# The first block's feed-forward layers: the first pair of column tiles as eight plain products instead of seven combined ones

## The chip, the core and the metric

The kernel runs on one core of a Trainium2 chip. That core has TensorE (PE in the profile; its weight loads are shown as PEld), VectorE (DVE), ScalarE (ACT), GpSimd (POOL) and SyncE (SP), which here only starts loads from the chip's memory. Each engine works through its own queue in order and waits on semaphores for the others. The metric is the time of one execution in microseconds on the device; less is better.

## The reference, cut to what matters

Two layers of a first block (attention of two kinds, each followed by a SwiGLU feed-forward layer), then a second block that the change doesn't touch. The sequence has 512 positions, the model 1024 columns, and the hidden layer of both feed-forward layers 2816.

```python
def rmsnorm(x, g):
    xf = x.astype(F32)
    y = xf * lax.rsqrt(jnp.mean(xf * xf, axis=-1, keepdims=True) + EPS)
    return (y * g.astype(F32)).astype(x.dtype)

def swiglu(h, w_gate, w_up, w_down):
    return (jax.nn.silu(h @ w_gate) * (h @ w_up)) @ w_down

    for layer in range(DEPTH):          # DEPTH = 2
        h = rmsnorm(x, attn_norm[layer])
        ...
        h = rmsnorm(x, ffn_norm[layer])
        x = x + swiglu(h, ffn_w_gate[layer], ffn_w_up[layer], ffn_w_down[layer])
```

## The kernel before, in words

Activations lie transposed: `x[0]` to `x[7]` are eight tiles of 128 model columns by 512 positions. The function `ffn(i, edge)` does one feed-forward layer, and is called for both layers (the first at some 293 us of the span, the second at some 926 us).

**Products.** The 22 column tiles of the hidden layer are taken in `NP = 11` pairs. For one pair the weights are a 2 x 2 matrix of blocks A11, A12, A21, A22: row one or two is the first or second tile of the pair, column one or two the first or second four of the eight model tiles. A block `wg[p, b]` (b = 0 to 3 in that order) has 128 x 1024 numbers, gate and up columns together. The activations are a 2 x 2 matrix too: B11 and B21 are the model tiles 0 to 3 and 4 to 7 for positions 0 to 255, B12 and B22 the same for positions 256 to 511. The plain way is eight block products. The kernel uses a scheme with seven (Winograd's form of Strassen's), which needs sums of weight blocks and of activation blocks: its products a to g use B11, B21, T1 = B12 - B11, T2 = B22 - T1, B22, T3 = B22 - B12 and T4 = B21 - T2, in that order.

**Split numbers.** Each f32 operand is split in a high part (a cast to fp32r on ACT, line 206, tiles `h` for weights and `t` for activations) and the rest (a subtraction on DVE, line 207, tiles `l` and again `t`). A block product (`product`, line 710) is three products of the parts: 24 matmuls of 128 x 128 by 256 columns. `scaled(q)` (line 741) makes the activation block `y[q]` from x, the norm's weights and the broadcast factor `edge.r` (named `rbc` in the profile): y0 to y3 are B11, B21, B12, B22. `parts4` splits such a block in four pieces.

**Order.** PE, DVE, ACT and SP run in an order that the code writes out (`manual_schedule`). `jobs` lists the products: a and b of the pairs 0, 1 and 2 (`AHEAD = 3`) come first, then c, d, e, f of pair 0, then c, g, d, e, f with the g of the pair before, and from pair 3 on also the products with the down weights (`D`). `ahead(n + 2)` splits the weights of a job two jobs early, `pre_c`, `post_c` and `pre_e` make the sums of weight blocks (lines 806 to 815), and the dictionary `turn` says at which job the sums of activations are made:

```python
            turn = {2: sum1, 3: sum2, 4: plain, 5: sum3, 6: sum4}
            also = {0: [lambda: edge.norm(1)], 1: [lambda: edge.spread(1)]}
```

`sum1` and `sum2` scale B12 and B22 first. `edge.norm(0)` and `edge.spread(0)` have made the norm's factor of the first 256 positions before `ffn` starts; `edge.norm(1)` and `edge.spread(1)` make that of the other 256 behind the first and the second product. `norm` sums squares with small matmuls (line 68, `sums`; squares of six tiles are added on POOL into `acc`, those of the last two come from ACT), goes through a few small instructions on DVE and ACT (lines 71 to 73, 224 to 234), and `spread` broadcasts the factor (line 79 on PE, line 80 on ACT). The results of c to g are put together on DVE in lines 873 to 889 (`m` is m5, `u`, `c`), and the matmuls of f add to the bank of d, so f waits until `u` has been made from it. SiLU and the gating of the pair's four quarters are `first` (`hq`) and `others` (`hr`).

Above `ffn` stands the output projection of the mixer (`pso`, lines 174 to 176 and 521), which adds to x, first for positions 0 to 255, then for 256 to 511. Its instructions, the squares and the first instructions of `ffn` (those in `high_priority`) are interleaved by the builder.

Of the kernel before, what the change touches and what calls it, by code (L numbers as in the profile page):

```python
# [8 lines left out]
F32 = mybir.dt.float32  # L9
# [73 lines left out]
class Net:  # L83
# [631 lines left out]
    def ffn(self, i, edge):  # L715
# [5 lines left out]
        with ExitStack() as st:  # L721
# [12 lines left out]

            y, T = [place("y") for _ in range(4)], []
# [8 lines left out]
            t = [None] * 4  # L744

            def sum1():
                scaled(2)
                t[0] = place("y")
                v_.tensor_sub(out=t[0], in0=y[2], in1=y[0])
                T.append(self.parts4(t[0], piece))  # L750

            def sum2():
                scaled(3)
                t[1] = place("y")
                v_.tensor_sub(out=t[1], in0=y[3], in1=t[0])
                T.append(self.parts4(t[1], piece))

            def plain():
                T.append(self.parts4(y[3], piece))

            def sum3():
                t[2] = place("y")
                v_.tensor_sub(out=t[2], in0=y[3], in1=y[2])
                T.append(self.parts4(t[2], piece))

            def sum4():
                t[3] = place("y")
                v_.tensor_sub(out=t[3], in0=y[1], in1=t[1])
                T.append(self.parts4(t[3], piece))

# [22 lines left out]

            p1, s1, m5, u, pa, pb, cs, hq, hr, done, ws, sm = ({} for _ in range(12))
            due = {}
# [24 lines left out]
            def split(job, p):  # L820
                if job == "D":
                    r, m, x0, x1 = p
                    ws[job, p] = parts(down.pop(p), 256 * (x1 - x0))
                    return
# [33 lines left out]


            def run(job, p):  # L860
                if job == "a":
                    p1[p] = bank("p1")
                    mm(p1[p], (job, p), 0, True)
                    s1[p] = w2.tile([128, S], F32, tag="s1", name="s1", bufs=3)
                    s_.copy(out=s1[p], in_=p1[p])
                elif job == "b":
                    mm(p1[p], (job, p), 1, False)
                    later(1, lambda: first(p))
                elif job == "c":
                    pb[p] = bank("pb")  # L870
                    mm(pb[p], (job, p), 2, True)
                    m5[p] = self.sm.tile([128, S], F32, tag="rq", name="m5", bufs=1)
                    s_.copy(out=m5[p], in_=pb[p])  # L873
                    later(1, lambda: v_.tensor_tensor(out=m5[p], in0=m5[p], in1=s1[p], op=ALU.add))
                elif job == "d":
                    pa[p] = bank("pa")
                    mm(pa[p], (job, p), 3, True)
                    u[p] = w2.tile([128, S], F32, tag="u", name="u", bufs=1)
                    v_.tensor_tensor(out=u[p], in0=s1[p], in1=pa[p], op=ALU.add)
                elif job == "e":  # L880
                    mm(pb[p], (job, p), 4, False)
                    cs[p] = w2.tile([128, 3, 2, 256], F32, tag="c", name="c", bufs=1)
                    v_.tensor_tensor(out=cs[p][:, 0], in0=two(u[p]), in1=two(pb[p]), op=ALU.add)
                elif job == "f":
                    mm(pa[p], (job, p), 5, False)
                    v_.tensor_tensor(out=cs[p][:, 2], in0=two(m5[p]), in1=two(pa[p]), op=ALU.add)  # L886
                elif job == "g":
                    mm(pa[p], (job, p), 6, False)
                    v_.tensor_tensor(out=cs[p][:, 1], in0=two(s1[p]), in1=two(pa[p]), op=ALU.add)
# [17 lines left out]

            jobs = [(j, p) for j in "ab" for p in range(AHEAD)]
            rounds = [(r, min(r + ROUND, NP)) for r in range(0, NP, ROUND)]
            D = iter([("D", (r, m, *r_)) for r, r_ in enumerate(rounds) for m in range(8)])  # L910
            for p in range(NP):
                if p < AHEAD:
                    order = "cGdef"
                else:
                    order = ("acGdbefDD", "aDcGDdDbeDf", "aDcDGdbef")[p % ROUND]
                for j in order:
                    if j == "D":
                        jobs.append(next(D))
                    elif j != "G":
                        jobs.append((j, p))  # L920
                    elif p:
                        jobs.append(("g", p - 1))
# [26 lines left out]
            trig = self.trig() if i == 0 else iter(())  # L949
            with self.tc.manual_schedule(engines={ET.PE, ET.DVE, ET.Activation, ET.SP}):  # L950
# [4 lines left out]
                for p in range(AHEAD):  # L955
                    load(0, p, early)
                first_raw = []
                for p in range(AHEAD):
                    r = pw.tile([128, 1024], F32, tag=f"r{2 + p // 2}", name="r", bufs=2)
                    raw[1, p] = r  # L960
                    nc.sync.dma_start(out=r, in_=wg[p, 1])
                for n in range(2):
                    ahead(n)
                for n, (j, p) in enumerate(jobs):
                    now[0] = n
                    for fn in due.pop(n, []):
                        fn()
                    if n == 3:
                        load(3, 0)
                        load(0, 0)  # L970
                        load(2, 0)
                    if n == 4:
                        load(1, 0)
                        load(2, 1)
                    if n == 5:
                        load(3, 1)
                    ahead(n + 2)
# [1056 lines left out]
```

## Time and profile before

| | us |
|---|---|
| median of 3 runs | 2052.57 (2052.55 to 2055.12) |
| the profiled execution | 2061.09 |
| its span, first to last instruction | 2059.4 |
| PE busy in the span | 1930.6 (94%) |
| DVE busy in the span | 1360.5 (66%) |
| mean granted TensorE clock | 0.966 |

A page of the profile gives busy times per engine; the timeline lists instructions with their start and, in brackets, how long the engine stood idle before and which instruction ended that. The granted clock is 1.00 at 2.4 GHz and 0.50 at 1.2 GHz. A wide matmul (256 columns) is shown with its whole duration, some 0.28 us, though the next starts 0.12 us later, so distances between starts are what counts on PE.

### The profile page before, as it was taken

What the parts mean: (1) busy time and instruction counts of PE and PEld (TensorE: products, weight loads), DVE (VectorE), ACT (ScalarE), POOL (GpSimd) and SP (SyncE); (2) the same over time, 40 slices, a digit from 0 to 9 for tenths busy, and PEclk for the clock granted to TensorE, in tenths of its full rate; (3) what the DMA queues carried; (4) which work ended last, traced back from release to release, by engine and by line L of the source; (5) the groups of instructions that cost most, each with busy time, mean ns of one, the idle gap of its engine ahead of it and who ended that gap; (6) DMA issues with size and microseconds to landing.
All of it is one profiled execution on the core that took longest, in us unless ns stands there. A gap on an engine that the chain in (4) does not pass through costs nothing. (4 is left out here: it accounts for less than half of the span.)

```text
span 2059.4 us, 29588 instructions
## 1 busy us (share of the span) xinstructions
PE 1930.6 (94%) x11604; PEld 1642.0 (80%) x11604; DVE 1360.5 (66%) x2294; ACT 895.1 (43%) x1532; POOL 425.8 (21%) x429
## 2 busy tenths in 40 slices
PE   9969987999999999996999999979989999999997
PEld 7736677899997867776899998768878788888886
DVE  6435658867677666557877675777848678666424
ACT  5435544434444455534434343534235545444321
POOL 2314310000001165420000000444424241111001
PEclk9979998999999999998999999989989999999998
DMA  4230023323232310113333231321210222232332
GB/s 159 70 67 20 28 105 103 131 85 120 76 103 67 96 55 23 34 58 122 119 108 121 75 108 52 111 88 67 72 52 2 78 69 95 99 98 97 94 93 70
DMA packets 57987, 169.38 MB, mean 82 GB/s; under 512 B 6288, under 2 KB 13368, under 8 KB 57848
## 3 DMA queue, kind: packets, MB, share of 16 engines
q1 hardware_dynamic: 54544, 162.51, 23.9%
q10 hardware_dynamic: 3224, 4.72, 1.1%
q8 instruction: 91, 1.49, 0.3%
q14 instruction: 48, 0.39, 0.1%
q0 software_dynamic: 80, 0.26, 0.0%
HBM read 161.70 MB, written 5.77 MB: 81 GB/s over the span
## 5 line engine op out<-in xcount | busy, mean ns | idle before, releaser
L168 ACT CAST whi<-raw 128x1024 fp32r<-128x1024 f32 (+3 forms) x146 | 144.4, 990 | 282.9 <-PE o L175 93.2
L169 DVE TENSOR_TENSOR wlo<-raw,whi 128x1024 fp32r<-128x1024 f32 (+3 forms) x138 | 165.6, 1200 | 128.5 <-ACT whi L168 128.0
L710 PE MATMUL pa<-t,h 128*128 128x256 f32 x1056 | 191.2, 283 | 9.6 <-DVE c L886 4.9
L710 PEld LDWEIGHTS pa<-t,h 128*128 128x128 f32 x1056 | 163.9, 190 | 13.1 <-issue 9.6
L1005 POOL TENSOR_TENSOR acc<-acc,sqt 128x256 f32<-128x256 f32 (+1 forms) x58 | 68.5, 1182 | 505.1 <-ACT sqt L1004 503.1
L207 DVE TENSOR_TENSOR l<-r,h 128x1024 fp32r<-128x1024 f32 x104 | 127.0, 1221 | 52.5 <-ACT h L206 52.0
L710 PE MATMUL pb<-t,h 128*128 128x256 f32 x704 | 134.9, 292 | 21.4 <-ACT m L873 11.6
L710 PE MATMUL pa<-t,l 128*128 128x256 f32 x528 | 149.1, 282 | 1.3 <-DVE l L207 1.3
L710 PE MATMUL p<-t,h 128*128 128x256 f32 x704 | 131.8, 288 | 8.4 <-ACT h L206 8.4
L206 ACT CAST h<-r 128x1024 fp32r<-128x1024 f32 x104 | 107.6, 1046 | 68.1 <-PE pd L175 20.5
L175 PE MATMUL o<-xl,whi 128*128 128x512 f32 (+1 forms) x352 | 134.5, 382 | 0.9 <-DVE xl L214 0.9
L174 PE MATMUL o<-xh,whi 128*128 128x512 f32 (+1 forms) x352 | 134.7, 383 | 0.0
L710 PEld LDWEIGHTS pb<-t,h 128*128 128x128 f32 x704 | 115.5, 200 | 23.2 <-ACT m L873 12.0
L176 PE MATMUL o<-xh,wlo 128*128 128x512 f32 (+1 forms) x352 | 133.9, 381 | 0.0
L176 PE MATMUL pd<-ah,l 128*128 128x512 f32 x320 | 127.3, 398 | 1.9 <-DVE l L207 1.9
L174 PE MATMUL pd<-ah,h 128*128 128x512 f32 x320 | 126.9, 397 | 0.3 <-ACT h L206 0.3
L175 PE MATMUL pd<-al,h 128*128 128x512 f32 x320 | 126.8, 396 | 0.0
L710 PEld LDWEIGHTS p<-t,h 128*128 128x128 f32 x704 | 112.6, 195 | 10.0 <-ACT h L206 8.8
L710 PE MATMUL p<-t,l 128*128 128x256 f32 x352 | 101.5, 288 | 2.7 <-DVE l L207 2.7
L710 PE MATMUL pb<-t,l 128*128 128x256 f32 x352 | 102.6, 291 | 0.9 <-DVE l L207 0.9
L710 PEld LDWEIGHTS pa<-t,l 128*128 128x128 f32 x528 | 100.5, 190 | 2.1 <-DVE l L207 2.1
L206 ACT CAST h<-raw 128x768 fp32r<-128x768 f32 (+2 forms) x70 | 55.6, 800 | 82.6 <-PE pd L175 60.8
(545 smaller groups left out, 5211.7 us busy)
## 6 DMA issues: line engine op xcount, KB each, us to landing
r<-w_gu SPq DMA_DIRECT2D x94, 512.0 KB, 3.6
raw<-w_gu SPq DMA_DIRECT2D x50, 512.0 KB, 3.6
raw<-w_dn SPq DMA_DIRECT2D x48, 384.0 KB, 4.0
raw<-w_in SPq DMA_DIRECT2D x22, 512.0 KB, 3.5
raw<-w_dn SPq DMA_DIRECT2D x16, 448.0 KB, 3.2
raw<-w_qka SPq DMA_DIRECT2D x8, 512.0 KB, 3.6
raw<-w_dn SPq DMA_DIRECT2D x16, 256.0 KB, 2.6
raw<-w_out SPq DMA_DIRECT2D x8, 512.0 KB, 3.8
```

The lines of the kernel that those rows point to most:

```text
L168: nc.scalar.copy(out=hi[:, :n], in_=raw[:, :n])
L169: (eng or nc.vector).tensor_sub(out=lo[:, :n], in0=raw[:, :n], in1=f(hi[:, :n]))
L174: mm(out, lh, rh, start=start, stop=False)
L175: mm(out, lh, rl, start=False, stop=False)
L176: return mm(out, ll, rh, start=False, stop=stop)
L206: self.nc.scalar.copy(out=hi, in_=src)
L207: (eng or self.nc.vector).tensor_sub(out=lo, in0=src, in1=f(hi))
L710: self.nc.tensor.matmul(c, l, r, start=first and n == 0, stop=k == 3 and n == 2, skip_group_check=True)
L1005: return nc.gpsimd.tensor_add(out=self.acc[:, c], in0=self.acc[:, c], in1=t)
```

## The change

Pair 0 is computed with the eight plain block products (job `q`), so that it needs only the blocks themselves. The first twelve jobs are now the eight products of pair 0 and a, b of the pairs 1 and 2; then c, d, e, f of pair 1 follow, and the order goes on as before. B12 and B22 are scaled and split at jobs 2 and 3, and the sums T1 to T4 at jobs 4, 6, 8 and 13. The split of the first two weight blocks is put ahead of the scaling of B11 and B21 inside `high_priority`, and the loads of weights are issued in the order of the new jobs (`fetch`).

```diff
-            own = iter([(pp, f"t{j}") for j in range(12)] + [(self.xp, f"x{n}{k}") for k in range(8) for n in "hl"])
+            own = [(pp, f"t{j}") for j in range(12)] + [(self.xp, f"x{n}{k}") for k in range(8) for n in "hl"]
+            own = iter(own + own[8:12])
...
+            def quadrant(n, q):
+                scaled(q)
+                T[n] = self.parts4(y[q], piece)
...
+            def term(n, x, z):
+                t[n] = place("y")
+                v_.tensor_sub(out=t[n], in0=x(), in1=z())
+                T[n] = self.parts4(t[n], piece)
...
+            def each(n):
+                if n == 0:
+                    hq[0] = w2.tile([128, 256], F32, tag="hq", name="hq", bufs=3)
+                elif 0 not in hr:
+                    hr[0] = w2.tile([128, 3, 256], F32, tag="hr", name="hr", bufs=1)
+                gated(hr[0][:, n - 1, :] if n else hq[0], quads[n][:, 0:256], quads[n][:, 256:512])
...
+                if job == "q":
+                    _, n, q, start = p
+                    if start:
+                        quads[n] = bank("c")
+                    mm(quads[n], (job, p), q, start)
+                    if not start:
+                        later(1, lambda: each(n))
+                        if n == 3:
+                            later(3, lambda: hidden(0))
...
-            jobs = [(j, p) for j in "ab" for p in range(AHEAD)]
+            jobs = [q("A11", 0, "B11", True), q("A21", 2, "B11", True), ("a", 1), ("a", 2),
+                    q("A12", 0, "B21", False), q("A22", 2, "B21", False), ("b", 1), ("b", 2),
+                    q("A11", 1, "B12", True), q("A21", 3, "B12", True), q("A12", 1, "B22", False), q("A22", 3, "B22", False)]
...
-            for p in range(NP):
-                if p < AHEAD:
+            for p in range(1, NP):
+                if p < 3:
                     order = "cGdef"
...
-            turn = {2: sum1, 3: sum2, 4: plain, 5: sum3, 6: sum4}
+            turn = {2: lambda: quadrant("B12", 2), 3: lambda: quadrant("B22", 3),
+                    4: lambda: term("T1", lambda: y[2], lambda: y[0]), 6: lambda: term("T2", lambda: y[3], lambda: t["T1"]),
+                    8: lambda: term("T3", lambda: y[3], lambda: y[2]), 13: lambda: term("T4", lambda: y[1], lambda: t["T2"])}
...
+            fetch = {0: [lambda: block(1, 2, None, 3)], 1: [lambda: block(0, 0, None, 3, "A11")],
+                     2: [lambda: load(0, 1), lambda: block(2, 0, None, 3, "A21"), lambda: load(2, 1), lambda: load(3, 1)],
+                     5: [lambda: load(3, 2)], 9: [lambda: load(1, 1)], 10: [lambda: load(2, 2)]}
...
                 with self.tc.high_priority(HP):
-                    for q in range(2):
-                        scaled(q)
-                        T.append(self.parts4(y[q], piece))
...
+                    for n in range(2):
+                        ahead(n)
+                    quadrant("B11", 0)
+                    quadrant("B21", 1)
```

The queues show three places where this moves work. On ACT, at the end of the first mixer's projection (x_78 to x_85 are x0 to x7; the squares feed the norm of positions 0 to 255), before:

```order
L1004 ACTIVATE sqt<-x_81 128x256
L1004 ACTIVATE sqt<-x_82 128x256
L1004 ACTIVATE sqt<-x_83 128x256
L60 ACTIVATE sqt<-x_84 128x256
L60 ACTIVATE sqt<-x_85 128x256
L1001 ACTIVATE acc<-x_78 128x256
```

and now:

```order
L1017 ACTIVATE sqt<-x_81 128x256
L206 CAST h<-raw 128x1024
L1017 ACTIVATE sqt<-x_82 128x256
L1017 ACTIVATE sqt<-x_83 128x256
L206 CAST h<-raw 128x1024
L60 ACTIVATE sqt<-x_84 128x256
L60 ACTIVATE sqt<-x_85 128x256
L1014 ACTIVATE acc<-x_78 128x256
```

The casts of the first two weight blocks stand among the squares; before, three such casts stood behind the four casts of B11 and B21. DVE's subtractions of the two blocks moved in the same way, among the additions to x. On DVE, behind the scaling of B22 in the first layer (y_2448 to y_2451 are y0 to y3; the names with s and raw or r are sums of weights and weights), before:

```order
L755 TENSOR_TENSOR y_2641<-y_2451,y_2588 128x1024
L207 TENSOR_TENSOR t_2644<-y_2641,t_2643 128x512
L207 TENSOR_TENSOR t_2648<-y_2641,t_2647 128x512
L207 TENSOR_TENSOR l_2682<-s_2635,h_2681 128x1024
L810 TENSOR_TENSOR s_2635<-s_2635,r_2627 128x1024
L811 TENSOR_TENSOR r_2629<-r_2627,r_2629 128x1024
L207 TENSOR_TENSOR t_2690<-y_2451,t_2689 128x512
L207 TENSOR_TENSOR t_2694<-y_2451,t_2693 128x512
L838 TENSOR_TENSOR hq_2675<-hq_2675,p1_2502 128x256
L207 TENSOR_TENSOR l_2727<-s_2635,h_2726 128x1024
L815 TENSOR_TENSOR r_2677<-r_2677,s_2635 128x1024
```

and now:

```order
L207 TENSOR_TENSOR t_2642<-y_2451,t_2641 128x512
L207 TENSOR_TENSOR t_2646<-y_2451,t_2645 128x512
L207 TENSOR_TENSOR l_2677<-r_2466,h_2676 128x1024
L753 TENSOR_TENSOR y_2680<-y_2450,y_2448 128x1024
L207 TENSOR_TENSOR t_2683<-y_2680,t_2682 128x512
L207 TENSOR_TENSOR t_2687<-y_2680,t_2686 128x512
L207 TENSOR_TENSOR l_2719<-raw_2500,h_2718 128x1024
L826 TENSOR_TENSOR hq_2714<-hq_2714,c_2506 128x256
L207 TENSOR_TENSOR l_2750<-raw_2549,h_2749 128x1024
L753 TENSOR_TENSOR y_2753<-y_2451,y_2680 128x1024
```

The sums of pair 0's weights (lines 806 to 815) are gone there, B22 itself is split first, and T1 and T2 come later. Further on in the same queue, ahead of the `u` of pair 1, which both kernels make, before:

```order
L883 TENSOR_TENSOR c_2880<-u_2846,pb_2784 128x512
L207 TENSOR_TENSOR l_2883<-r_2625,h_2882 128x1024
L886 TENSOR_TENSOR c_2880<-m5_2809,pa_2821 128x512
L207 TENSOR_TENSOR l_2914<-s_2819,h_2913 128x1024
L815 TENSOR_TENSOR r_2772<-r_2772,s_2819 128x1024
L874 TENSOR_TENSOR m5_2943<-m5_2943,s1_2576 128x512
L207 TENSOR_TENSOR l_2947<-r_2772,h_2946 128x1024
L889 TENSOR_TENSOR c_2880<-s1_2527,pa_2821 128x512
L207 TENSOR_TENSOR l_2980<-r_2679,h_2979 128x1024
L806 TENSOR_TENSOR s_2985<-r_2817,r_2886 128x1024
L879 TENSOR_TENSOR u_3012<-s1_2576,pa_2987 128x512
L838 TENSOR_TENSOR hr_2977<-hr_2977,c_2880 128x768
```

and now:

```order
L826 TENSOR_TENSOR hr_2747<-hr_2747,c_2835 128x256
L207 TENSOR_TENSOR l_2961<-r_2861,h_2960 128x1024
L826 TENSOR_TENSOR hr_2747<-hr_2747,c_2869 128x256
L879 TENSOR_TENSOR m5_2991<-m5_2991,s1_2631 128x512
L207 TENSOR_TENSOR l_2996<-r_2586,h_2995 128x1024
L791 TENSOR_TENSOR s_3001<-r_2894,r_2716 128x1024
L753 TENSOR_TENSOR y_3003<-y_2449,y_2753 128x1024
L207 TENSOR_TENSOR t_3006<-y_3003,t_3005 128x512
L207 TENSOR_TENSOR t_3010<-y_3003,t_3009 128x512
L884 TENSOR_TENSOR u_3038<-s1_2631,pa_3013 128x512
L836 TENSOR_TENSOR al_3041<-hq_2714,ah_3040 128x256
```

T4 now stands right ahead of `u`, the three `c` of pair 0 are gone, and the gating of pair 0's other three quarters is done in three small steps (two of them above) ahead of `u` instead of one behind it.

## Rows read from the trace of the kernel before

**Rows 1.** Stretches of the first layer: length, busy per engine, granted clock, DMA share, GB/s.

```profile
293.00:362.00 69.00, 50.84 (x353) 48.83 (x351) 53.66 (x72) 29.05 (x44) 2.02 (x2) 0.85 0.34 116
362.00:400.00 38.00, 34.66 (x284) 33.95 (x285) 33.57 (x39) 19.00 (x25) 0.00 (x0) 1.00 0.39 132
400.00:660.00 260.00, 259.13 (x1718) 237.02 (x1717) 185.19 (x213) 102.25 (x131) 4.20 (x3) 1.00 0.28 91
```

**Rows 2.** Whom PE waited for, 293 to 400 us: total, times, longest.

```profile
PE pb L710 <- ACT m L873: 5.8, 1, 5.8
PE pb L710 <- ACT h L206: 4.9, 1, 4.9
PE p L710 <- ACT h L206: 4.6, 1, 4.6
```

**Rows 3.** Timeline of PE, first layer.

```profile
292.96 0.28 PE L176 MATMUL pso<-oh,wl 128*128 128x256 f32 x1
...
308.62 0.59 PE L79 MATMUL sums<-dg,ones 128*128 128x256 f32 x2
...
346.32 0.40 PE L710 MATMUL pa<-t,h 128*128 128x256 f32 x2
...
349.19 0.40 PE L710 MATMUL pb<-t,h 128*128 128x256 f32 x2
```

**Rows 4.** Timeline of ACT, both layers: small steps of the norm, casts, squares.

```profile
286.47 0.20 ACT L224 ACTIVATE rst<-v 128x2 f32<-128x2 f32 x1 [0.17 <-DVE v L71]
...
296.20 0.62 ACT L206 CAST t<-y 128x512 fp32r<-128x512 f32 x1 [0.17 <-DVE y L741]
296.73 2.94 ACT L206 CAST h<-raw 128x1024 fp32r<-128x1024 f32 x3
299.57 0.72 ACT L60 ACTIVATE sqt<-x 128x256 f32<-128x256 f32 x2
...
914.79 0.42 ACT L1004 ACTIVATE sqt<-x 128x256 f32<-128x256 f32 x1 [0.40 <-POOL acc L1005]
...
928.51 0.62 ACT L206 CAST t<-y 128x512 fp32r<-128x512 f32 x1 [0.17 <-DVE y L741]
```

**Rows 5.** The second weight block's load: issue in both layers, landing in the first.

```profile
279.94 0.33 SPq L784 DMA_DIRECT2D raw<-w_gu  x1
...
DMA to landing us min/median/max: 4.2/4.2/4.2
...
911.43 0.33 SPq L784 DMA_DIRECT2D raw<-w_gu  x1
```

**Rows 6.** Timeline of DVE, first layer, behind the `u` of pair 1.

```profile
362.04 0.95 DVE L838 TENSOR_TENSOR hr<-hr,c 128x768 f32<-128x768 f32 x1
```

**Rows 7.** Scaling of B12 to the end of pair 1's `u`, both layers; columns as in rows 1.

```profile
311.80:362.04 50.24, 37.37 (x267) 35.91 (x265) 41.73 (x53) 20.58 (x29) 0.00 (x0) 0.86 0.29 96
943.71:993.95 50.24, 36.93 (x267) 35.44 (x265) 41.73 (x52) 20.57 (x29) 0.00 (x0) 0.86 0.28 94
```

**Rows 8.** DVE in that stretch of the first layer, by form: busy, mean ns | idle before, releaser.

```profile
L207 DVE TENSOR_TENSOR l<-r,h 128x1024 fp32r<-128x1024 f32 x7 | 8.6, 1222 | 5.1 <-ACT h L206 5.0
L207 DVE TENSOR_TENSOR t<-y,t 128x512 fp32r<-128x512 f32 x10 | 6.5, 686 | 2.7 <-ACT t L206 2.7
...
L879 DVE TENSOR_TENSOR u<-s,pa 128x512 f32<-128x512 f32 x2 | 1.4, 678 | 0.0
L838 DVE TENSOR_TENSOR hq<-hq,p 128x256 f32<-128x256 f32 x3 | 1.2, 413 | 0.0
```

**Rows 9.** Timeline of PE around the first sums of squares, second layer.

```profile
915.63 0.28 PE L176 MATMUL pso<-oh,wl 128*128 128x256 f32 x1
...
917.81 0.36 PE L174 MATMUL pso<-oh,wh 128*128 128x256 f32 x1
```

**Rows 10.** Two short stretches of the second layer; columns as in rows 1.

```profile
918.00:924.00 6.00, 6.00 (x38) 5.82 (x38) 4.31 (x12) 2.16 (x7) 2.20 (x3) 0.72 0.01 4
1000.00:1002.00 2.00, 0.00 (x0) 0.00 (x0) 2.00 (x4) 0.00 (x0) 0.00 (x0) 1.00 0.54 213
```

More of the change, by code (lines that the diff above doesn't have):

```diff
@@ L732, in piece @@
                 return p_.tile([128, 2, 256], F32R, tag=tag, name="t")
-            y, T = [place("y") for _ in range(4)], []
+            y, T = [place("y") for _ in range(4)], {}
             def scaled(q):
@@ L742, in scaled @@
                                             in1=edge.r[:, c], op0=ALU.mult, op1=ALU.mult)
[L744 to L769, printed above, removed]
+            def quadrant(n, q):
+                scaled(q)
+                T[n] = self.parts4(y[q], piece)
+            t = {}
+            def term(n, x, z):
+                t[n] = place("y")
+                v_.tensor_sub(out=t[n], in0=x(), in1=z())
+                T[n] = self.parts4(t[n], piece)
             ring = self.turns({"h": [(self.wp, "whi", 2)] * 2 + [(pw, "whi", W3)] * W3,
@@ L791, in parts @@
                 return hi, lo
-            p1, s1, m5, u, pa, pb, cs, hq, hr, done, ws, sm = ({} for _ in range(12))
+            p1, s1, m5, u, pa, pb, cs, hq, hr, done, ws, sm, quads = ({} for _ in range(13))
             due = {}
@@ L823, in split @@
                     ws[job, p] = parts(down.pop(p), 256 * (x1 - x0))
+                    return
+                if job == "q":
+                    ws[job, p] = parts(raw[p[0]])
                     return
@@ L857, in others @@
                 gated(hr[p], cs[p][:, :, 0, :], cs[p][:, :, 1, :])
-            def run(job, p):
-                if job == "a":
+            def each(n):
[4 more added lines that the diff above has]
+                gated(hr[0][:, n - 1, :] if n else hq[0], quads[n][:, 0:256], quads[n][:, 256:512])
+            def run(job, p):
+                if job == "q":
+                    _, n, q, start = p
[6 more added lines that the diff above has]
+                            later(3, lambda: hidden(0))
+                elif job == "a":
                     p1[p] = bank("p1")
-                    mm(p1[p], (job, p), 0, True)
+                    mm(p1[p], (job, p), "B11", True)
                     s1[p] = w2.tile([128, S], F32, tag="s1", name="s1", bufs=3)
@@ L866, in run @@
                 elif job == "b":
-                    mm(p1[p], (job, p), 1, False)
+                    mm(p1[p], (job, p), "B21", False)
                     later(1, lambda: first(p))
@@ L880, in run @@
                 elif job == "e":
-                    mm(pb[p], (job, p), 4, False)
+                    mm(pb[p], (job, p), "B22", False)
                     cs[p] = w2.tile([128, 3, 2, 256], F32, tag="c", name="c", bufs=1)
@@ L947, in ffn, with block @@
             also = {0: [lambda: edge.norm(1)], 1: [lambda: edge.spread(1)]}
-            turn = {2: sum1, 3: sum2, 4: plain, 5: sum3, 6: sum4}
+            turn = {2: lambda: quadrant("B12", 2), 3: lambda: quadrant("B22", 3),
+                    4: lambda: term("T1", lambda: y[2], lambda: y[0]), 6: lambda: term("T2", lambda: y[3], lambda: t["T1"]),
+                    8: lambda: term("T3", lambda: y[3], lambda: y[2]), 13: lambda: term("T4", lambda: y[1], lambda: t["T2"])}
             trig = self.trig() if i == 0 else iter(())
+            def block(b, p, tag, n, key=None):
+                r = early() if tag is None else pw.tile([128, 1024], F32, tag=f"r{tag}", name="r", bufs=n)
+                raw[key or (b, p)] = r
+                nc.sync.dma_start(out=r, in_=wg[p, b])
+            fetch = {0: [lambda: block(1, 2, None, 3)], 1: [lambda: block(0, 0, None, 3, "A11")],
+                     2: [lambda: load(0, 1), lambda: block(2, 0, None, 3, "A21"), lambda: load(2, 1), lambda: load(3, 1)],
+                     5: [lambda: load(3, 2)], 9: [lambda: load(1, 1)], 10: [lambda: load(2, 2)]}
             with self.tc.manual_schedule(engines={ET.PE, ET.DVE, ET.Activation, ET.SP}):
                 with self.tc.high_priority(HP):
-                    for q in range(2):
-                        scaled(q)
-                        T.append(self.parts4(y[q], piece))
[L955 to L963, printed above, removed]
+                    block(0, 0, None, 3, "A11")
+                    block(2, 0, None, 3, "A21")
+                    block(0, 1, None, 3)
+                    block(0, 2, 0, 1)
+                    block(1, 0, 1, 1, "A12")
+                    block(3, 0, 2, 2, "A22")
+                    block(1, 1, 3, 2)
+                    for n in range(2):
+                        ahead(n)
+                    quadrant("B11", 0)
+                    quadrant("B21", 1)
                 for n, (j, p) in enumerate(jobs):
@@ L967, in ffn @@
                         fn()
[L968 to L976, printed above, removed]
+                    for fn in fetch.get(n, []):
+                        fn()
                     ahead(n + 2)
```

11 lines of the change are left out of this document (6 added, 5 removed).

## The prediction

> **What bounds the kernel now.** The stretches come first [rows 1]. From 400 us to the end of the first layer PE is busy 259.13 of 260 us at the full clock: there PE is the bound, and nothing that another engine does counts. From 293 to 362 us it is busy only 50.84 of 69 us and its clock is 0.85, while DVE is busy 53.66; from 362 to 400 us PE is busy 34.66 of 38, DVE 33.57. So the time to be won lies in the first hundred microseconds of each layer, and the view of waits says where: three long ones, 4.6 us before the first product and 4.9 and 5.8 us before later ones, all on something that ACT has still to cast [rows 2]. ACT is no bottleneck (29.05 of 69 us): its casts of sums come late because DVE makes those sums. The second layer repeats this: the stretch from the scaling of B12 to the end of pair 1's `u` is 50.24 us long with DVE busy 41.73 in both layers [rows 7]. The product f of pair 1 waits for that `u`. I therefore sum up to there: when does B12's scaling begin, and how long is the stretch behind it?
>
> **What is added on PE.** One product per layer. A product is 2.87 us (346.32 to 349.19) at the full clock [rows 3], so 5.7 us in both layers; at half the clock twice that. This is paid only where PE is the bound. Up to f of pair 1 it isn't: PE has 14 products from the second on, 40 us, and DVE's stretch alone is longer.
>
> **Term A, when B12's scaling begins.** Four steps.
> (1) The early casts. ACT takes its queue in order, and the second cast now stands ahead of the last two squares. Its load is issued at 279.94 and lands 4.2 us later [rows 5], at 284.1; a cast takes 0.98 us (2.94 for three) [rows 4], DVE's subtraction 1.22 [rows 8], so DVE is free at 286.3. Two additions and two squares (0.7 for two [rows 4]) stand behind it, so the norm's step `rst`, at 286.47 before, runs at 287.4: 0.95 us later. In the second layer the load is issued at 911.43 and lands near 915.7; with its cast the square that ran at 914.79 runs at 916.8. POOL, behind which that square waited before, takes back 0.4 of the 2.0: 1.6 us later. Price: 0.95 and 1.6 us on everything behind it, PE's projection included.
> (2) Then B11 and B21 are scaled and cast as before; the last of those casts, 296.20 to 296.8, ends at 297.8. Behind it stands one weight cast instead of three (0.98 instead of 2.94), then the two squares (0.72): ready at 299.4 instead of 300.3 [rows 4].
> (3) The first product needs no cast that is still to come, so it starts when the projection ends (292.96 before [rows 3], some 294 now), is through by 297, and PE waits for the squares. The second product runs from 299.85 (behind the sums, 0.4 us) to 302.7. The small steps of the norm, 1.7 us, hide under it.
> (4) From `spread` on PE (308.62 before [rows 3]) to the scaling of B12 (311.80 [rows 7]) it is 3.2 us: broadcast, one weight cast, one subtraction, all there as before. So 305.9 instead of 311.80: **5.9 us earlier**. In the second layer the same chain, later by the difference of step 1, gives **5.3**.
>
> The clock is the open point of step 3. The rows that show it are the nearest I have: in the second layer PE went 2.2 us between wide matmuls (915.63 to 917.81) with only the norm's small ones in it [rows 9], and the next 6 us had a clock of 0.72 [rows 10], which is 3.4 us at 0.50 and a loss of 1.7. A wait of 2 us at 1000 left the clock at 1.00 [rows 10]. The new gap, 297 to 299.85 with small matmuls in it, lies nearer to the first. So the second product may take 4.6 us instead of 2.9, and A loses 1.7 in that layer. I take this for one layer of the two, as the two rows part.
>
> The Trainium skill has a rule on this, in "TensorE: Matmul & The Clock Gate", Part 1: "the default state is throttled, and activity releases the throttle." Read strictly, an engine that is never long without work keeps its full rate, and since the long waits go, no product of the first thirty would run at the lower one; the total below would then be 21.4 us, without the 1.7. The trace agrees only in part: the long waits were followed by the lower clock (0.85 over the stretch [rows 1]), and so was the short gap of rows 9.
>
> **Term B, DVE's stretch from there to the end of `u`.** By the queue: the sums of weights are fewer by four of 128 x 1024 (pair 0 needs none of its four; `T` sums stay four), one weight subtraction more (11 instead of 10): net three fewer at 1.22 us. Two more piece subtractions (12 instead of 10) at 0.69. Five fewer additions from the accumulators (two `c`-`m`-`u` kinds instead of seven) at 0.68. Three more gatings of a quarter at 0.41 [rows 8]. That is -3.66 + 1.38 - 3.40 + 1.23 = -4.45; three instructions fewer, each of which overlaps its neighbour by 0.08, make it **-4.2**. DVE's idle time in the stretch is 50.24 - 41.73 = 8.5 us [rows 7], nearly all of it waits for the casts of what it has itself just made or for weight casts behind those [rows 8]. The new order has the same pattern (cast on ACT, subtraction on DVE), so I keep 8.5. Its bounds: nothing, if every cast is ready (-8.5 us more per layer; PE would still not be the bound), and 25 us, if each of the 11 weight subtractions waits 1.9 us, as much as the longest single waits, and each of six sums of activations 0.7 (2.7 for four [rows 8]).
>
> **Term C.** Behind `u` stood the gating of pair 0's three quarters, 0.95 us [rows 6]; it is now done earlier. DVE is still full there (33.57 of 38 [rows 1]), so **-0.9**. What follows is the same queue in both kernels.
>
> **Edits at no cost.** SP issues more loads early, in another order: the four behind the projection follow each other, and the weights for the fifth product are needed at 303.7, nine microseconds after their issue; a load lands in 4.2 [rows 5], and if the cover were gone each microsecond would delay a product by one. T4's pieces reuse those of B12, whose two products end before T4 is made. One more weight cast and two more piece casts on ACT (2.2 us) lie in its idle time (half the stretch); without it they would fall on DVE's waits, as in the upper bound above.
>
> **Sum.** First layer -5.9 - 4.2 - 0.9 = -11.0, second -5.3 - 4.2 - 0.9 = -10.4, one fall of the clock +1.7: -19.7 us. From 400 us on PE is the bound and does the same work, so nothing of this is lost or won later. Made against the profiled execution (2061.09 us, span 2059.4) it gives 2041.4; the runs' median, 2052.57, is 8.5 lower, and the stretches lie inside the span, so I take the difference from it: **2032.9 us**.
>
> **Rivals.**
> *Waits shrink too.* With twelve plain jobs ahead, casts may be ready; half of the 8.5 us gone in both layers gives 2032.9 - 8.5 = 2024. For it: weight blocks wait for no sums in the first eight jobs. Against it: T1 to T3 and B12, B22 still go from DVE to ACT and back. Chance 0.11.
> *Part of it is given back.* The twelve products need eight weight splits in a row, each behind a cast; if DVE waits 4.5 us more per layer, half as much again as before: 2032.9 + 9 = 2042. For it: PE waits there for `u`, which T4 now precedes. Chance 0.15.
> *Slower: DVE waits for each cast.* The place is DVE's stretch; it decides when idle time rises from 8.5 to over 19 us per layer (8.5 + 11.0, less the fall). At the upper bound of 25 us each layer is 5.5 to 6 us slower: 2064. For it: 16 instead of 14 weight and sum splits stand in that stretch. Against it: the same kind of wait averaged 0.7 us before (5.1 over seven [rows 8]). Chance 0.04.
> *It doesn't do what it says.* If the first product still started at 298 because the early splits were late, the squares would be late as well, term A would go, and T would come no earlier; B and C leave 10 us, less the added 5.7 where PE then is the bound: 2048. Chance 0.02.
>
> **The numbers.** The forecast itself has 0.68: 0.38 with one fall of the clock, 0.18 with none (2052.57 - 21.4 = 2031.2, the case of the long waits alone) and 0.12 with two (2034.6). What a measurement of this kernel can tell from no change is about 0.2%, 4 us. Faster: 0.68 + 0.11 + 0.14; the same 0.03; slower 0.04. The range goes from the middle of the first rival, 2025, to that of the second, 2042.5.
>
> **What the changed profile would show.** Step 1: `rst` near 287.4, the first product some 1 us behind the projection instead of 4.9. Step 4: B12 scaled from 305.9. Term B: 46 us from there to the end of `u`, DVE busy 37.5. The waits of 4.9 and 5.8 us gone, one wait of 3 to 5 us in front of f of pair 1 in their place. From 400 us on the same rows, 10 to 11 us earlier. I am wrong if DVE's stretch keeps its 50 us, or if ACT's squares wait longer for the early casts than 1.6 us.

## The result, and the profile after

| | us |
|---|---|
| changed kernel, median of 11 runs | 2047.15 (2043.21 to 2051.36) |
| kernel before, median of 11 runs | 2059.44 (2052.55 to 2065.96) |
| ratio | 0.9942, 95% interval 0.9926 to 0.9958 |
| profiled execution of the changed kernel | 2044.56, span 2042.8, clock 0.970 |

The kernel is about 12 us faster (9 to 15 by the interval); 19.7 us were forecast. The absolute time is further off than that: the three runs that the forecast started from (2052.57) lay at the fast end of what the kernel before does, whose runs scatter over 13 us. The two profiled executions differ by 16.5 us, some 4 us more than the medians, which is chance of the same kind.

The stretches of the first layer after the change (they answer to [rows 1]; columns as there):

```profile
293.00:362.00 69.00, 58.42 (x438) 56.25 (x438) 56.40 (x77) 32.97 (x50) 0.87 (x1) 0.93 0.39 137
362.00:400.00 38.00, 37.69 (x286) 35.98 (x285) 30.84 (x35) 17.07 (x22) 0.00 (x0) 1.00 0.41 137
400.00:660.00 260.00, 256.86 (x1689) 233.72 (x1688) 187.99 (x219) 106.05 (x137) 7.59 (x5) 1.00 0.28 89
...
305.82:351.91 46.09, 36.70 (x291) 34.70 (x289) 37.63 (x50) 23.66 (x36) 0.00 (x0) 0.99 0.26 90
931.58:977.65 46.07, 37.70 (x291) 36.31 (x289) 37.62 (x50) 23.65 (x36) 0.00 (x0) 0.96 0.26 89
```

PE is now busy 58.42 of the first 69 us instead of 50.84. The last two rows run from the scaling of B12 to the end of pair 1's `u`: 46.1 us, DVE busy 37.6, as forecast (46 and 37.5), against [rows 7]. Whom PE waited for from 290 to 400 us (answering to [rows 2]), and the first rows of the products:

```profile
PE pa L710 <- DVE u L884: 4.2, 1, 4.2
PE p L710 <- ACT h L206: 2.1, 1, 2.1
PE p L710 <- DVE l L207: 1.5, 2, 0.8
PE sums L68 <- ACT sqt L60: 1.0, 1, 1.0
```

```profile
292.82 0.28 PE L176 MATMUL pso<-oh,wl 128*128 128x256 f32 x1
292.93 0.40 PE L710 MATMUL c<-t,h 128*128 128x256 f32 x2
...
352.06 0.77 PE L710 MATMUL pa<-t,h 128*128 128x256 f32 x2 [4.23 <-DVE u L884]
```

The three long waits are gone, the first product starts right behind the projection, and f of pair 1 waits 4.2 us for `u`. So far the forecast holds. That B12 is scaled at 305.82, where 305.9 was forecast, is luck, though: the first addition of the projection's last products to x ran at 275.44 instead of 277.47, so 2.0 of these 6.0 us lie ahead of the changed code. What the forecast missed is largest in the second layer, inside the projection. The timeline of POOL and DVE there, then PE's waits, then the stretch behind them:

```profile
900.48 1.60 POOL L1018 TENSOR_TENSOR acc<-acc,sqt 128x256 f32<-128x256 f32 x2 [19.57 <-ACT sqt L1017]
902.82 1.39 POOL L1018 TENSOR_TENSOR acc<-acc,sqt 128x256 f32<-128x256 f32 x1 [0.74 <-ACT sqt L1017]
904.29 1.71 POOL L1018 TENSOR_TENSOR acc<-acc,sqt 128x256 f32<-128x256 f32 x1
...
902.40 1.23 DVE L207 TENSOR_TENSOR l<-raw,h 128x1024 fp32r<-128x1024 f32 x1 [1.07 <-ACT h L206]
...
904.21 1.22 DVE L207 TENSOR_TENSOR l<-raw,h 128x1024 fp32r<-128x1024 f32 x1
```

```profile
PE sums L68 <- POOL acc L1018: 3.0, 1, 3.0
PE sums L68 <- ACT sqt L60: 1.6, 1, 1.6
```

```profile
908.00:914.00 6.00, 6.00 (x28) 5.86 (x27) 2.06 (x8) 1.30 (x5) 1.45 (x2) 0.50 0.01 4
```

Two of POOL's additions of squares take 1.39 and 1.71 us where the two ahead of them took 0.8 each, PE waits 3.0 us for them, and the next 6 us of the projection run at half clock. (The wait of 1.6 us is that for the other half's squares, behind the first product.) For the comparison of all kernels I measure four stretches between instructions that all of them have: **a** from the first addition of the projection's last products to x (L521, positions 0 to 255) to the scaling of B11; **b** from there to the scaling of B12; **c** from there to the first result of the down projection; **d** from that in the second layer to the first instruction on DVE that uses the next block's broadcast factor (`pb<-psr,rbc`). Slashes part the layers. Each row is one execution.

| kernel | a | b | c | d |
|---|---|---|---|---|
| before | 12.4 / 11.9 | 21.9 / 21.7 | 96.0 / 96.0 | 290.6 |
| changed | 13.6 / 18.0 | 16.8 / 16.9 | 90.8 / 90.7 | 292.8 |
| changed_again | 14.8 / 15.6 | 16.8 / 16.9 | 90.8 / 90.8 | 293.1 |
| late_splits | 12.0 / 11.4 | 20.7 / 25.4 | 90.8 / 90.8 | 293.2 |
| early_alone | 13.8 / 16.9 | 16.9 / 18.6 | 96.0 / 96.2 | 290.9 |
| second_late | 14.5 / 12.4 | 19.3 / 19.5 | 90.8 / 90.8 | 293.1 |
| t4_later | 13.8 / 13.3 | 16.8 / 16.9 | 91.5 / 91.0 | 292.2 |
| sub_late | 12.8 / 15.0 | 20.8 / 25.4 | 90.8 / 90.8 | 293.2 |
| filler | 13.3 / 14.8 | 15.3 / 18.5 | 90.8 / 90.8 | 293.1 |
| b21_behind | 12.2 / 11.7 | 16.9 / 17.0 | 90.8 / 90.8 | 293.6 |
| b21_ring | 12.0 / 11.5 | 16.9 / 17.0 | 90.8 / 90.8 | 293.0 |
| ring_turn | 12.9 / 17.5 | 15.3 / 18.5 | 90.8 / 90.7 | 293.0 |
| b21_ring_d | 12.4 / 11.8 | 16.9 / 17.1 | 90.8 / 90.8 | 292.3 |
| seven_b21 | 11.8 / 13.4 | 17.4 / 17.5 | 96.0 / 96.2 | 291.4 |

Stretch c repeats within 0.1 us where pair 0 has plain products and T4 its place, and within 0.3 us with seven products. Stretches a and b repeat within 0.4 us in the three b21 kernels with plain products, whose clock never fell there. That is what makes single executions comparable, though their total times scatter by several us. Stretch d repeats less well: 292.2 to 293.6 in the eight executions that differ in nothing behind c.

### The profile page after: what moved, and what is told of

Same layout as the page of the kernel before. It is cut to its first block, busy times and chain, and to the rows that moved or that the text cites. A ratio compares the mean times of both kernels' runs of the same rounds, so it can differ in the third digit from the quotient of the medians.

```text
span 2042.8 us, 29679 instructions
## 1 busy us (share of the span) xinstructions
PE 1931.4 (95%) x11652; PEld 1645.2 (81%) x11652; DVE 1349.0 (66%) x2286; ACT 896.6 (44%) x1538; POOL 428.5 (21%) x429
## 5 line engine op out<-in xcount | busy, mean ns | idle before, releaser
L710 PE MATMUL pa<-t,h 128*128 128x256 f32 x960 | 177.3, 286 | 10.3 <-DVE u L884 8.4
L710 PEld LDWEIGHTS pa<-t,h 128*128 128x128 f32 x960 | 152.1, 193 | 12.7 <-ACT ah L835 8.7
L710 PE MATMUL pa<-t,l 128*128 128x256 f32 x480 | 137.4, 286 | 1.9 <-DVE l L207 1.9
L710 PE MATMUL p<-t,h 128*128 128x256 f32 x640 | 117.8, 284 | 4.1 <-ACT h L206 4.1
L710 PE MATMUL pb<-t,h 128*128 128x256 f32 x640 | 115.9, 282 | 0.0
L710 PEld LDWEIGHTS p<-t,h 128*128 128x128 f32 x640 | 100.5, 191 | 6.0 <-ACT h L206 4.5
L710 PEld LDWEIGHTS pb<-t,h 128*128 128x128 f32 x640 | 99.8, 191 | 1.0
L710 PEld LDWEIGHTS pa<-t,l 128*128 128x128 f32 x480 | 93.0, 194 | 2.7 <-DVE l L207 2.7
L710 PE MATMUL p<-t,l 128*128 128x256 f32 x320 | 91.0, 284 | 3.0 <-DVE l L207 3.0
L710 PE MATMUL pb<-t,l 128*128 128x256 f32 x320 | 90.4, 283 | 1.1 <-DVE l L207 1.1
```

The costliest lines, as they stand in the source:

```text
L710: self.nc.tensor.matmul(c, l, r, start=first and n == 0, stop=k == 3 and n == 2, skip_group_check=True)
```

## The experiments

**late_splits, early_alone: the two halves of the change.** In late_splits the first two weight splits go back behind the scaling of B11 and B21; early_alone is the kernel before with the loads and these splits moved ahead of it.

The edit of late_splits:

```diff
-                    for n in range(2):
-                        ahead(n)
                     quadrant("B11", 0)
                     quadrant("B21", 1)
+                for n in range(2):
+                    ahead(n)
```

> The changed kernel with the first two weight splits put back behind the scaling of B11 and B21; all else as changed. Theory 1 (the trace of the changed kernel): the early casts push the norm back inside the projection and cost PE a stretch at half clock, so of term A only some 3.6 us are won in the first layer and nothing in the second. Then this kernel scales B12 about 3.6 us later than the changed one in the first layer and at the same distance from the projection in the second; the 46.1 us behind it stay; the time is 3 to 4 us above the changed kernel, 8 to 9 below the kernel before. Rival, the prediction's own term A: 5.9 and 5.3 us go with the early casts, so the time is 10 to 11 us above the changed kernel and about that of the kernel before, less 2. In both, PE waits 4 to 5 us again ahead of the first product.

> The kernel before (seven products for every pair, sums as they were) with the loads and the first two weight splits put ahead of the scaling of B11 and B21. Theory 1: B12 is scaled some 3.6 us earlier in the first layer and not earlier in the second, the 50.2 us behind it stay, so 3 to 5 us faster in all (0.998). Rival, term A as predicted: 5.9 and 5.3 us earlier, 9 to 11 us faster (0.995). Either way the wait of 4.6 us ahead of the first product goes and a wait of 1 to 2 us for the squares takes its place.

Measured: late_splits 2054.0 us, ratio to the kernel before 0.9969 (0.9949 to 0.9989); early_alone 2059.14, 0.9988 (0.9969 to 1.0006). Stretch c of 90.8 comes with the plain products alone and a of 13.6 and more with the early splits alone, so the two halves are cleanly parted. The early splits alone are worth 2.5 us by the ratio (from 6 us faster to 1 slower), near theory 1; beside the plain products they are worth the difference of the ratios, 0.0027 or some 6 us, between theory 1 and the rival. Neither said why: in the second layer of late_splits PE's wait for the first cast (4.4 us, as in its first layer) cost more than before, since the clock stayed low from there to B12:

```profile
923.00:937.00 14.00, 13.10 (x61) 12.89 (x62) 5.84 (x11) 3.64 (x7) 0.00 (x0) 0.52 0.50 171
```

**second_late, t4_later.** One has only the first weight split early (`ahead(1)` behind the scaling of B21), the other makes T4 at job 15 instead of 13.

> The changed kernel with only the first weight split early; the second stands behind the scaling of B21, after the casts of B21. Theory 1: in the second layer the norm of positions 0 to 255 comes 1.5 to 2.5 us earlier than in the changed kernel (its distance from the end of the mixer), the stretch at half clock in the projection may go (3.4 us); against that the two squares ahead of the second product come 1 us later in both layers. Net 0 to 4 us faster than the changed kernel. Rival: the casts don't matter and the stretches at half clock are chance: 1 to 2 us slower, by the later squares.

> The changed kernel with T4 made at job 15 (f of pair 1) instead of 13, so that u of pair 1 no longer stands behind T4's three instructions on DVE. Theory 2: PE's wait of 4.2 us ahead of f of pair 1 is DVE's queue; the three instructions and the wait between them take 3.1 us, so u ends 3.1 us earlier, the wait falls to about 1 us and what follows comes 3 us earlier in each layer, 6 us in all, and up to 5 more if the stretch at half clock behind the wait goes too: 2036 to 2041 us. Rival: DVE is full behind u as well (9.81 of 10 us), so the next product that needs a split or T4 itself (g of pair 1) waits instead and the time stays within 2 us of the changed kernel.

second_late: 2046.16 us, 0.9932 (0.9911 to 0.9954), not to be told from the changed kernel. Stretch a of the second layer came back to 12.4, b grew by 2.5 in both layers, more than the 1 us forecast: in the first layer PE waited 2.4 us for the squares instead of 1.0, and from 302.1 to 308.9 us its clock was 0.50. t4_later: 2045.29 us, 0.993 (0.991 to 0.9951), the same. The rival is right, and the waits show how:

```profile
PE pa L710 <- DVE c L891: 4.2, 1, 4.2
...
PE pa L710 <- DVE u L884: 1.0, 1, 1.0
```

f waits 1.0 us instead of 4.2, and g, behind the `c` that T4 now precedes on DVE, waits the 4.2: stretch c is not shorter (91.5 and 91.0). DVE's queue is the bound up to these products, and a wait of PE in it can be moved but not won. (From 362 to 400 us it is PE that is full: 37.69 of 38 us in the rows above.)

**sub_late, filler, changed_again: what delays the norm in the projection.** sub_late casts the first two weight blocks early but subtracts them on DVE behind B21; filler gives PE 24 matmuls, whose result nothing uses, ahead of the norm's sums in the second layer.

```diff
+                if len(rest) < 2:
+                    s_.copy(out=hi, in_=t)
+                    rest.append(lambda: v_.tensor_sub(out=lo, in0=t, in1=hi.bitcast(F32)))
...
+                        for n in range(FILL if w == "w_mo" else 0):
+                            self.nc.tensor.matmul(edge.sums[:, 256:512], ws[0][0][:, 0:128], oh[7][:, HALVES[0]], start=True, stop=True, skip_group_check=True)
                         edge.norm(0)
```

> The changed kernel with the first two weight blocks cast early as now, but their subtractions on DVE put behind B21's. Theory 3 (POOL's additions of squares slow down while DVE subtracts 1024 columns): in the second layer all additions of 256 columns take 0.72 to 0.95 us, none 1.4 or 1.7, and the norm's sums come 1.3 to 2 us earlier than in the changed kernel, while the first product waits some 4 us for its second operand. Rival (the casts in ACT's queue alone are late): additions of 1.4 us appear all the same, or none, and the norm's sums come no earlier than in the changed kernel.

> The changed kernel with 24 matmuls of 256 columns, whose result nothing uses, put on PE ahead of the norm's sums in the second layer's projection, where PE waited 3.0 us. Theory 4 (that wait is what lets the clock fall to half in the rest of the projection): the clock stays at 1.00 there, the 6.8 us at half clock go and B11 is scaled 1 to 2.5 us earlier in the second layer; behind the first product nothing changes. Rival: the clock falls all the same (the waits behind it, or chance), and the time is that of the changed kernel or up to 1 us more.

> The changed kernel once more, unchanged. If the long way from the projection to B11's scaling in the second layer (17.97 us against 11.87 before) is a matter of the order, it comes again within 1 us; if it is chance of clock and loads, it lies between 13 and 18.

POOL's additions in sub_late, second layer:

```profile
908.03 1.57 POOL L1026 TENSOR_TENSOR acc<-acc,sqt 128x256 f32<-128x256 f32 x2 [21.86 <-ACT sqt L1025]
910.25 2.33 POOL L1026 TENSOR_TENSOR acc<-acc,sqt 128x256 f32<-128x256 f32 x3 [0.65 <-ACT sqt L1025]
```

All five take 0.72 to 0.75 us, with short gaps between those shown as one row, and theory 3 holds: from the first addition to x to the first step behind the norm's sums it is 9.8 us, against 12.7 in the changed kernel and 11.3 in changed_again (7.8 before; one execution each). Of the 3.5 to 4.9 us of delay 2.0 are the casts in ACT's queue, the rest (1.5 to 2.9) the subtractions. But PE still waited for POOL, and the projection still ran at half clock behind that:

```profile
PE sums L68 <- POOL acc L1026: 2.8, 1, 2.8
```

```profile
912.00:919.00 7.00, 6.37 (x30) 6.37 (x31) 1.65 (x7) 2.19 (x7) 1.78 (x3) 0.52 0.01 2
```

So the early casts alone are enough for this wait and this fall, and stretch a is 15.0 there, not the 11.9 of the kernel before. The first product waited 5.7 us for its second operand, so this single run took 2061.69 us. In filler PE did not wait there and the clock stayed up in the projection, as theory 4 says, but it fell behind it:

```profile
908.00:912.00 4.00, 4.00 (x33) 3.77 (x33) 3.09 (x8) 1.80 (x5) 1.46 (x2) 1.00 0.00 2
912.00:917.50 5.50, 4.18 (x37) 4.10 (x36) 5.50 (x11) 2.96 (x7) 2.15 (x2) 1.00 0.60 198
918.00:924.80 6.80, 6.80 (x32) 6.80 (x33) 3.34 (x8) 1.52 (x4) 0.00 (x0) 0.50 0.85 318
```

PE had waited 1.7 us for the squares just before. a gave 0.8 to 3.2 us, b took 1.6 back; the interval of the ratio, 0.9892 to 0.9935 around 0.9914 (2042.33 us), overlaps the changed kernel's. Its first layer, whose code is unchanged, ran without a fall: b is 15.3 there against 16.8, so the fall of some 3 us that the changed kernel has in b costs 1.5 us, and the longer one above 3.2 (18.5). The wait for the squares was there all the same:

```profile
PE sums L68 <- ACT sqt L60: 1.4, 1, 1.4
```

```profile
299.00:303.00 4.00, 4.00 (x34) 3.95 (x34) 2.03 (x5) 1.98 (x3) 0.00 (x0) 1.00 0.99 355
```

changed_again (2045.88) leaves its question half open: a of the second layer is long again, 15.6 against 11.9 before, so a delay belongs to the order; but it is 2.4 us shorter than 18.0, so by the terms set beforehand its size is partly chance.

**b21_behind, seven_b21: no split in the projection.** B11 is scaled, then the first two weight blocks are split, and B21, first needed by the fifth product, follows at job 1. seven_b21 does the same in the kernel before, with the loads left where they stood there. The edit of b21_behind:

```diff
-                    for n in range(2):
-                        ahead(n)
                     quadrant("B11", 0)
-                    quadrant("B21", 1)
+                for n in range(2):
+                    ahead(n)
...
-            turn = {2: lambda: quadrant("B12", 2), 3: lambda: quadrant("B22", 3),
+            turn = {1: lambda: quadrant("B21", 1), 2: lambda: quadrant("B12", 2), 3: lambda: quadrant("B22", 3),
```

> The changed kernel with no weight split inside the projection and with B21 scaled and split later: B11 is scaled, then the first two weight blocks are split, then the norm of the other half runs, and B21 follows behind the second split of weights that the order does anyway (job 1); B21 is first needed by the fifth product. Theory 1 (the early splits cost the norm in the projection 1.2 us in the first layer and 1.5 to 6 in the second, B21's scaling costs nothing there): the distance from the first addition of the projection's last half to B11's scaling is 12.0 to 12.5 us again, from there to B12's scaling 16.5 to 17.5, behind that 90.8 to the first result of the down projection as in the changed kernel: 1 us less in the first layer and 5 to 6 less in the second, 2037 to 2041 us. Rival: DVE's queue ahead of B12 is full, so the 3.4 us of B21 stand on the path and the distance from B11's to B12's scaling is 20 us: no gain over the changed kernel, or 2 us slower.

> The kernel before, with seven products for every pair, but with its first two weight splits ahead of B21's scaling, which moves to job 1 as in the version with B21 later. Nothing is split inside the projection. If the parts add up, this has the early start alone: from B11's to B12's scaling some 17 us instead of 21.8 in both layers, the 96.0 us behind it as in the kernel before, and 290.6 to 291 to the next block's broadcast: 9 to 10 us below the kernel before (0.9955), and 8 us above the version with B21 later, which is then what the plain products bring (5.2 us a layer, less 2.3 us at the end of the second). Rival: without the plain products the third product's split (a of pair 2) and the sums behind it hold PE up, and less than half of it is won.

b21_behind: 2040.3 us, 0.9901 (0.9881 to 0.992), which lies wholly below the changed kernel's 0.9926 to 0.9958. a is back at 12.2 and 11.7, b stays near 17, at full clock:

```profile
292.00:303.00 11.00, 10.74 (x89) 10.68 (x90) 9.12 (x18) 5.54 (x11) 2.41 (x2) 1.00 0.97 365
```

So the early start can be had without the delay. That b is not 15.3, as without a fall in filler, is probably B21's 3.1 us on DVE, which now stand in b. seven_b21: 2051.45, 0.9956 (0.9937 to 0.9974), as expected: the early start alone is worth 9 us, and the plain products 11 more by the ratios, 8 by the stretches (5.2 and 5.4 of c, less 2.2 of d), within the intervals.

**b21_ring, ring_turn, b21_ring_d: the end of the second layer.** Split weights go round three buffers, two of which (`whi`, `wlo` of the pool `wp`) the next block uses for its first weights. One product more shifts the round. These kernels leave one slot out in the second layer, at job 79 (b21_ring, which is b21_behind with that; ring_turn is the changed kernel with that) or at job 88 (b21_ring_d, with 29 in place of the 26 below).

```diff
+            own3 = lambda n: [(self.wp, n, 2)] * 2 + [(pw, n, W3)]
+            slots = lambda n: own3(n) * 26 + own3(n)[1:] + own3(n) * 20 if i else own3(n)
+            ring = self.turns({"h": slots("whi"), "l": slots("wlo")})
```

> The version with B21 scaled later (no split inside the projection), and in the second layer one slot left out of the round of three buffers for split weights, so that the last three splits end on the buffers that they ended on before. Theory 5 (one more product per layer shifts the round, so that the last two products of the layer hold both buffers which the next block's first weights need; that is the 1.6 us from the first to the last result of the down projection that the second layer has lost, 265.18 against 263.62): this stretch falls to 263.6 and the second block starts 1.5 to 2 us earlier: 2037.5 to 2039 us. Rival: the late first cast of the next block has another cause (the order of loads): 265.2 stays, and the time with it.

> The changed kernel with only that slot left out of the round of buffers in the second layer. Theory 5: from the first to the last result of the second layer's down projection 263.6 us instead of 265.2, and the first cast of the next block's weights three to four us earlier against the last of these results. Rival: 265.2, as it was.

> The version with B21 scaled later, and the slot left out of the second layer's round of buffers at another place, job 88, where the product that runs in between is one of the down projection (18 matmuls of 512 columns, some 4.2 us) and so leaves time for the split that has to wait. Theory 5, mended: the first wait (1.3 us of PE where the slot was left out before) goes, the next block's first casts come as early as in the run before, and from the first result of the down projection to the next block's first broadcast it is 291 to 291.8 us instead of 293.0 to 293.6: about 1.5 to 2.5 us below the version with B21 later, 2037 to 2038.5 us. Rival: the loss is not the buffers' but the order of the block's first loads and additions, and 293 stays.

b21_ring: 2039.05 us, 0.991 (0.9893 to 0.9927); ring_turn 2045.16 (one run); b21_ring_d: 2037.17, 0.9898 (0.9873 to 0.9924), the lowest median, though its ratio can't be told from b21_behind's. Theory 5 failed in its number: from the first to the last result of the second layer's down projection it grew from 265.2 to 265.7 instead of falling to 263.6, since the results behind the missing slot came 1.3 us later, as PE waited there. At job 88 only two results came late and the others caught up, and the end shows in PE's waits from the changed kernel (first two rows) to b21_ring_d:

```profile
PE psr L175 <- DVE xl L214: 3.8, 1, 3.8
PE psr L176 <- DVE wlo L169: 0.9, 1, 0.9
```

```profile
PE psr L175 <- DVE xl L214: 2.4, 2, 2.2
```

Stretch d is 292.3 instead of b21_behind's 293.6, and 291 to 291.8 were forecast; but d is 292.2 in t4_later too, where the round is unchanged, so this difference alone shows nothing. What repeats is the part from the first to the last result: 265.16 to 265.19 in all eight executions with plain products and the unchanged round, 263.6 to 263.7 in the three with seven products, and 264.5 in b21_ring_d. So 0.7 of these 1.6 us are the buffers'. The rest is not explained; the rival's cause, the order of the additions around it, was not tried by itself.

## Why the prediction was off

Stretch by stretch, the forecast's terms against the mean of the two executions of the changed kernel:

| stretch, both layers | forecast | measured |
|---|---|---|
| a (step 1 of term A) | 0.95 + 1.6 = +2.6 | +1.8 + 4.9 = +6.7 |
| b (rest of term A, one fall of the clock) | -6.85 - 6.9 + 1.7 = -12.1 | -5.2 - 4.7 = -9.9 |
| c (terms B and C) | 2 x -5.1 = -10.2 | -5.2 - 5.2 = -10.4 |
| d (nothing lost later) | 0 | +2.4 |
| sum | -19.7 | -11.2 |

- **Right:** terms B and C, to 0.2 us, and with them that the extra product of each layer is hidden; the new wait in front of f; and steps 2 to 4 of term A, where the clock held: b of 15.3 in filler's first layer is what they give (21.9 - 6.85 = 15.1).
- **Failed, step (1):** "POOL, behind which that square waited before, takes back 0.4 of the 2.0: 1.6 us later." In the second layer nothing was taken back: the casts cost 2.0 up to the norm's sums (sub_late). The two subtractions, which the forecast left out there, cost another 1.5 to 2.9, and with them POOL's additions were stretched. PE's wait for POOL then brought the half clock into the projection, which the casts alone do too (sub_late) and which stays away where PE is kept busy (filler). The whole step was 3.7 and 6.1 us in the second layer of the two executions instead of 1.6, and 1.2 and 2.4 in the first instead of 0.95. late_splits and b21_behind show that all of it goes with the early splits (a of 11.4 to 12.2).
- **Mis-sized, the clock:** "I take this for one layer of the two." It fell behind the first product in both layers of both executions, 1.5 us each; the changed kernel's rows first, then changed_again's:

```profile
300.00:303.00 3.00, 3.00 (x16) 2.91 (x14) 1.23 (x2) 0.00 (x0) 0.00 (x0) 0.50 1.03 400
924.00:927.00 3.00, 3.00 (x17) 3.00 (x17) 2.50 (x8) 1.34 (x3) 0.00 (x0) 0.54 1.00 403
...
299.10:302.40 3.30, 3.30 (x17) 3.30 (x17) 2.39 (x7) 1.34 (x3) 0.00 (x0) 0.50 1.00 386
923.70:927.00 3.30, 3.30 (x18) 3.30 (x17) 1.90 (x4) 0.73 (x1) 0.00 (x0) 0.50 1.03 408
```

Waits of 1.0 to 1.7 us, with the norm's small matmuls beside them, stood ahead of these falls. In the first layer of filler and of ring_turn, whose code there is the changed kernel's, a wait of 1.4 us stood at the same place and the clock stayed at 1.00; so the order alone doesn't decide it, and what does stays open. The rule of the Trainium skill that the prediction quotes ("TensorE: Matmul & The Clock Gate", Part 1), read strictly as there, gave no fall; these four rows go against that reading.
- **Failed, "nothing of this is lost or won later":** 2.4 us were lost at the end of the second layer, 0.7 of it through the buffers' round (b21_ring_d); the cause of the rest is open. The number of products changes which buffer the last one holds; the forecast looked at times only.
- **The base:** 2052.57 was 6.9 us below the median of the 11 runs (2059.44), so even a right sum would have given too low a time. With the sum of the stretches, 11.2, the measured base gives 2048.2, near the 2047.15. Either miss alone would have left the time inside the forecast's range of 2025 to 2042.5: its sum from the measured base gives 2039.7, the measured sum from its base 2041.4.

## What to carry to other kernels

In this kernel a split that was moved early cost more than its own duration: name what stands behind it in ACT's queue, and which of POOL's operations run while DVE subtracts. Before moving work ahead of a chain, ask whether something in that place can go behind instead: B21 was not needed for four products, and moving it back won what moving the splits forward had lost. Where buffers go round and the number of users changes, look at who holds which buffer when the next stage begins.

## What the runs showed of the hardware

An addition on POOL (256 columns, two inputs) took mostly 0.72 to 0.79 us, but the two in the rows above that met a subtraction of 1024 columns on DVE took 1.39 and 1.71. The first ended at 904.21, 0.58 us after DVE's subtraction (902.40 + 1.23 = 903.63); the second at 906.00, 0.57 us after the other (904.21 + 1.22 = 905.43). It looks as if POOL did nothing until DVE was through. In the second layer of changed_again two additions took 1.39 and 1.38 us, in filler 1.40 and 1.60; in sub_late, without the subtractions, none did. The other order is there too, in filler:

```profile
902.02 0.74 POOL L1020 TENSOR_TENSOR acc<-acc,sqt 128x256 f32<-128x256 f32 x1
...
902.07 1.78 DVE L207 TENSOR_TENSOR l<-raw,h 128x1024 fp32r<-128x1024 f32 x1
```

The subtraction that began 0.7 us before the end of POOL's addition took 1.78 us instead of 1.22. The Trainium skill, "SBUF — State Buffer", section "Who interferes with whom", says that a VectorE instruction with two inputs in SBUF contends with a GpSimd instruction that reads SBUF, over a pair of ports that is an exclusive lock, and that the order of issue decides who blocks; these rows agree.
